# A decoder trunk layer in f32: the work up to the first Strassen pair in one fixed order on four engines, x transposed ahead of its modulation, w_ada summed two channel tiles at a time

## The chip, the cores and the metric

The kernel runs on one core of a Trainium2 chip. The core has TensorE (matrix products into PSUM banks), VectorE and ScalarE (elementwise work), GpSimd and SyncE, which here mostly issue loads and stores (SyncE the loads of weights and x, GpSimd small loads and the stores). In the profile they are PE (and PEld for its weight loads), DVE, ACT, POOL and SP. The metric is the device time of one execution in microseconds, as a median of several runs. Each profile belongs to one execution more, whose own time is given beside its span.

## What is computed

One layer, 1024 positions by 1024 channels, all in float32. Cut to what matters:

```python
mod = (c_act @ w_ada + b_ada)[:, None, :]
shift, scale, gate = jnp.split(mod, 3, axis=-1)
u = layer_norm(x) * (1 + scale) + shift
proj = u @ w_in + b_in
a_v, a_g, b_b, b_c, b_h, b_g, c_a, c_b, c_g, merge = jnp.split(proj, SPLIT_IDX, axis=-1)
...                       # three branches: pooling, short conv, conformer conv of 31 taps
h_c = causal_dwconv(c_a * jax.nn.sigmoid(c_b), cf_w, cf_b)
...
m = sum of sigmoid(merge_k) * (y_k @ w_branch[k])
return layer_norm(ALPHA * x + gate * (m @ w_out), ln_g, ln_b)
```

Everything starts at u: each of the 96 column tiles of the projection needs all of u, and u needs the normalised x and the first two thirds of c_act @ w_ada.

## The kernel before

**Precision.** A float32 product is made of three TensorE products of a coarser kind: an operand is split in a high half (a cast, `fp32r`) and a low half (the operand less its high half). `mm3` (L118) then adds low x high, high x low and high x high into one bank. So each operand costs a cast and a subtraction, "hi" and "lo" below. The cast is usually on ScalarE and the subtraction on VectorE (`split`, L109 to L111).

**u.** Channels lie on partitions. `ut[k]` is channel tile k (of 8) of the transposed, modulated x: 128 channels by 1024 positions, in two halves h of 512. `make_u` (L285) transposes four x tiles on TensorE into a bank (L288), and ScalarE writes `ut` from the bank with scale and bias of the modulation (L293). `split_u` (L297) makes hi (L301 on ScalarE, or L303, a cast on VectorE, by the table `HI_ACT`) and lo (L304) of it in `ub[k, h]`. The transposes and the small products of the modulation share two PSUM banks (`misc_ps`).

**The modulation.** `ada_load` brings w_ada in four pairs of channel tiles (a0, a2, a4, a6 in `LOADS`), each as four buffers of 512 KB. `ada_sum(k)` (L247) adds the eight row tiles, each times its c_act column, for one channel tile k: two starts on ScalarE (L257) and the rest on VectorE (L260, 256 columns, since shift and scale lie side by side). `ADA_PE` hands four of the eight rows of tile 0 to TensorE. `ada_mod(k)` (L270) sums over partitions with a product with ones (L276) and adds b_ada (L281).

**Jobs.** The projection's column tiles are jobs. The first four are *classic* jobs (class `Job`): 16 parts each (8 channel tiles, 2 halves), a part being one `mm3`, so 192 matmuls of 512 columns in all. All others are *pairs* (class `Pair`, L381): two column tiles at once as one step of Strassen-Winograd in seven products of twelve matmuls, A11·B11, A12·B21, S1·T1, S2·T2, S3·T3, S4·B22 and A22·T4. The S and A sides come from the weights (`prepare`, L398: four sums on VectorE and the splits wa, wb, wc, wd). The T sides are sums of quarters of u (`sum_u`, L308): four subtractions in place on `ut` (L312 to L315) and two splits, for each of four i. They can't begin before every split of those `ut` has been made. The first pair has the name b (its banks px_b, py_b, pz_b; its weights wa_b to wd_b), the next ones d and cg.

**The conv.** The two classic column-tile pairs end in `cs` (L482, L489), the input of the conformer conv: 30 instructions on VectorE for each of eight channel tiles (L519, the taps), six of them issued per job (`TAPS`).

**What sets the order.** `START` is a list of steps: l and n statistics and normalisation of an x tile, a and m the sum and the end of a modulation, u and v `make_u` and `split_u`, s a job's splits, p parts. It is read under `tc.manual_schedule(engines=PIN)` with `PIN` holding GpSimd alone. The other engines' orders are drawn by a scheduler while the kernel is built, from the order in the code and the dependencies, and are fixed from then on. Each engine works through its own list in that order and waits where an operand or a buffer isn't ready. The fourth classic job, the T sums and the first pair's splits follow START in the code (`ahead`, and `sum_u` ahead of the loop over jobs). Loads on SyncE's queue go in the order of `LOADS`, each as soon as its buffer is free; weights have four buffers (`RAW_BUFS`).

Of the kernel before, what the change touches and what calls it, by code (L numbers as in the profile page):

```python
# [46 lines left out]
def kernel(  # L47
# [117 lines left out]
    bin_cols = columns("bin_cols", [rows_of(b_in[0])], nc.gpsimd)  # L165
# [8 lines left out]
    vec_cols = columns("vec_cols", [a for _, a in names], nc.gpsimd)  # L174
# [11 lines left out]
    for i in range(2):  # L186
        sl = slice(i * nr, (i + 1) * nr)
        columns(f"cfw{i}", [cfw[sl, :]], nc.gpsimd, cfw_cols[:, sl])


    def rstd_of(name, var, n=1):
        r = small.tile([P, n], F32, tag=f"rstd{n}", name=name)
        nc.vector.tensor_scalar_add(r, var, EPS)
        nc.gpsimd.tensor_tensor(out=r, in0=r, in1=neg_half[:, :n], op=ALU.pow)
        return r
# [10 lines left out]

    def ln0_load(i):
        xn[i] = slot(f"x{i}")
        nc.sync.dma_start(out=xn[i], in_=x[i * P : (i + 1) * P, :])

    ln0_r = {}

    def ln0_stats(i):
        mv = stats_of(f"x{i}", xn[i])
        ln0_r[i] = mv, rstd_of(f"r{i}", mv[:, 1:2])

    def ln0(i):
        t, (mv, r) = xn[i], ln0_r[i]
        if i < 4:
            nc.vector.tensor_scalar(  # L220
                out=t, in0=t, scalar1=mv[:, 0:1], scalar2=r, op0=ALU.subtract, op1=ALU.mult
            )
            return
        nmr = small.tile([P, 1], F32, tag="nmr", name=f"nmr{i}")
        nc.vector.tensor_scalar(
            out=nmr, in0=mv[:, 0:1], scalar1=r, scalar2=-1.0, op0=ALU.mult, op1=ALU.mult
        )
        nc.scalar.activation(t, t, AF.Identity, bias=nmr, scale=r)
# [3 lines left out]
    def ada_load(k):  # L232

        for q in range(4):
            t = slot(f"ada{q}_{k}").rearrange("p (s k c) -> p s k c", s=2, c=2 * P)
            for s in range(2):
                marks["ada"] = nc.sync.dma_start(
                    out=t[:, s], in_=ada_src[:, s, 2 * q : 2 * q + 2, k * P : (k + 2) * P]
                )
            for e in range(2):  # L240
                raws.setdefault(k + e, []).extend(
                    t[:, :, i, e * P : (e + 1) * P] for i in range(2)
                )

    ada_acc = {}

    def ada_sum(k):  # L247

        raw, on_pe = raws[k], ADA_PE[k]
        parts = [(raw[kk], c_act[:, kk : kk + 1]) for kk in range(on_pe)]  # L250
        acc = []
        if on_pe < NT:
            both = slot(f"acc{k}").rearrange("p (n s c) -> p n s c", s=2, c=P)
        for kk in range(on_pe, NT):
            if len(acc) < 2:
                acc.append(both[:, len(acc)])
                nc.scalar.activation(acc[-1], raw[kk], AF.Identity, scale=c_act[:, kk : kk + 1])  # L257
            else:
                a = acc[(kk - on_pe) % 2]
                nc.vector.scalar_tensor_tensor(  # L260
                    out=a, in0=raw[kk], scalar=c_act[:, kk : kk + 1], in1=a,
                    op0=ALU.mult, op1=ALU.add,
                )
# [4 lines left out]
    mods = {}

    def ada_mod(k):  # L270

        ps = misc_ps(f"mod{k}")
        parts = ada_acc[k]
# [7 lines left out]
        nc.vector.tensor_add(mods[k], ps[:, :2], b)  # L281

    ut, ub = {}, {}

    def make_u(k, h):  # L285
        ps = misc_ps(f"tr{k}_{h}")
        for i in range(4):
            nc.tensor.transpose(  # L288
                ps[:, i * P : (i + 1) * P], xn[4 * h + i][:, k * P : (k + 1) * P], ident
            )  # L290
        if k not in ut:
            ut[k] = slot(f"ut{k}")
        nc.scalar.activation(  # L293
            ut[k][:, HALVES[h]], ps, AF.Identity, bias=mods[k][:, 0:1], scale=mods[k][:, 1:2]
        )

    def split_u(k, h):  # L297
        ub[k, h] = pair_slot(f"u{k}_{h}")
        hi, lo, t = ub[k, h][:, 0], ub[k, h][:, 1], ut[k][:, HALVES[h]]
        if HI_ACT[2 * k + h]:  # L300
            nc.scalar.activation(hi, t, AF.Identity)  # L301
        else:
            nc.vector.tensor_copy(out=hi, in_=t)  # L303
        marks["u"] = nc.vector.tensor_tensor(out=lo, in0=t, in1=f32(hi), op=ALU.subtract)  # L304
# [688 lines left out]
```

## Time and profile before

| | |
|---|---|
| median of the runs | 1421.26 us (3 runs, 1419.3 to 1421.34) |
| the profiled execution | 1417.33 us, its span 1415.6 us |
| busy in the span | PE 1335.6 (94%), DVE 1094.5 (77%), ACT 522.0 (37%), POOL 115.5 (8%) |
| mean granted TensorE clock | 0.986 |
| HBM read, written | 137.59 MB, 50.34 MB |

Two rows of the page show the span in 40 slices of 35.4 us. Each digit is the share of the slice in which the engine was busy, in tenths:

```profile
PE   2859999999999999999999999999998999999997
DVE  5589999999899769957985898699554757635576
```

TensorE is busy nine tenths and more in nearly every slice; the exceptions are the first three and a few later ones. VectorE is as busy as TensorE from the fourth slice to about the eleventh. The page adds busy times over stages that differ, so the prediction reads the first 230 us by themselves.

### The profile page before, as it was taken

To read this page: it belongs to the slowest core of one execution; us is meant where nothing else is said; L and a number is where in the kernel's file an instruction comes from. 1 tells how busy PE (TensorE), PEld (TensorE's weight loads), DVE (VectorE), ACT (ScalarE), POOL (GpSimd) and SP (SyncE) were. 2 spreads that over 40 slices of the span, in tenths; PEclk is the share of its full clock that TensorE was granted. 3 is DMA by queue.
4 is the path that set the end of the run, shared out by engine and by line. 5 is a ranking of instruction groups with operands and counts; after the bars stand their busy time and mean duration, and the time that the engine had idled before them with its cause. 6 is when DMAs were issued, how large, how long until landed. Compare 5 with 4: busy or idle time off the path is not lost.

```text
span 1415.6 us, 15312 instructions
## 1 busy us (share of the span) xinstructions
PE 1335.6 (94%) x5917; PEld 1100.9 (78%) x5917; DVE 1094.5 (77%) x1300; ACT 522.0 (37%) x654; POOL 115.5 (8%) x229
## 2 busy tenths in 40 slices
PE   2859999999999999999999999999998999999997
PEld 1647878888788878887888788877777888888886
DVE  5589999999899769957985898699554757635576
ACT  3453434443434434443444434344522333302200
POOL 3000000000000000000000000000211232200010
PEclk9989999999999999999999999999999999999998
DMA  9510222433312323221343224322777979812322
GB/s 333 148 45 16 75 89 90 134 107 102 119 60 75 104 75 104 77 89 44 105 149 104 80 76 133 113 89 82 272 273 275 333 270 359 288 63 64 130 102 92
DMA packets 168793, 188.92 MB, mean 133 GB/s; under 512 B 6420, under 2 KB 139616, under 8 KB 168720
## 3 DMA queue, kind: packets, MB, share of 16 engines
q1 hardware_dynamic: 142976, 95.43, 22.9%
q0 software_dynamic: 25696, 92.50, 17.4%
q8 instruction: 46, 0.75, 0.2%
q14 instruction: 27, 0.22, 0.0%
q10 hardware_dynamic: 48, 0.01, 0.0%
HBM read 137.59 MB, written 50.34 MB: 133 GB/s over the span
## 4 chain that ended last, share of the span: by engine, by line
PE 83%; issue 6%; DVE 5%; DMA 4%; ACT 2%; POOL 0%; SPq 0%; DVEq 0%; ACTq 0%; POOLq 0%
PE ps_z L120 17%; PE px_m L120 7%; PE px_d L120 6%; PE out_ps L120 6%; PE px_b L120 6%; PE px_a L120 5%; PE px_c L120 4%; PE pz_m L120 3%; PE px_cg L120 3%; PE pz_d L120 3%; PE pz_b L120 3%; PE ps_p L120 3%; PE pz_a L120 3%; PE pz_c L120 2%; DVE h L519 2%
## 5 line engine op out<-in xcount | busy, mean ns | idle before, releaser
L519 DVE SCALAR_TENSOR_TENSOR h<-r_c,cfw_cols,h 128x1023 f32<-128x1023 f32 (+9 forms) x180 | 227.1, 1262 | 5.1 <-ACT h L517 4.4
L741 DVE TENSOR_TENSOR g<-ps_z,g 128x512 f32<-128x512 f32 x48 | 31.8, 686 | 63.1 <-PE ps_z L120 62.5
L519 DVE SCALAR_TENSOR_TENSOR h<-cs,cfw_cols,h 128x1023 f32<-128x1023 f32 (+29 forms) x60 | 75.7, 1262 | 2.8 <-ACT h L517 2.3
L120 PE MATMUL ps_p<-u,w_p 128*128 128x512 f32 x192 | 52.6, 428 | 21.6 <-ACT cs L482 15.4
L110 ACT ACTIVATE w_z<-raw_z 128x1024 fp32r<-128x1024 f32 x24 | 25.2, 1060 | 123.2 <-PE ps_z L120 60.1
L120 PEld LDWEIGHTS ps_p<-u,w_p 128*128 128x128 f32 x192 | 37.9, 205 | 31.5 <-ACT cs L482 15.8
L111 DVE TENSOR_TENSOR w_z<-raw_z,w_z 128x1024 fp32r<-128x1024 f32 x24 | 29.1, 1220 | 18.7 <-ACT w_z L110 18.7
L120 PE MATMUL px_m<-u,wa_m 128*128 128x512 f32 x144 | 34.9, 390 | 2.5 <-DVE wa_m L111 2.5
L120 PE MATMUL ps_z<-y_1h,w_z 128*128 128x512 f32 x96 | 34.4, 394 | 2.0 <-ACT y_1h L115 2.0
L120 PE MATMUL px_m<-t_1h,wb_m 128*128 128x512 f32 x96 | 31.9, 392 | 4.5 <-ACT r_m L436 4.5
L120 PE MATMUL py_m<-u,wa_m 128*128 128x512 f32 x144 | 35.9, 389 | 0.0
L454 POOL DMA_DIRECT2D y_dram<-r_d x8 | 4.3, 539 | 379.4 <-DVE r_d L615 379.4
L120 PE MATMUL ps_z<-y_0h,w_z 128*128 128x512 f32 x96 | 35.2, 401 | 0.0
L120 PE MATMUL pz_m<-u,wc_m 128*128 128x512 f32 x144 | 35.1, 389 | 0.0
L120 PE MATMUL ps_z<-y_2h,w_z 128*128 128x512 f32 x96 | 33.9, 390 | 0.0
L120 PE MATMUL ps_z<-y_3h,w_z 128*128 128x512 f32 x96 | 33.7, 390 | 0.0
L120 PEld LDWEIGHTS px_m<-u,wa_m 128*128 128x128 f32 x144 | 27.0, 188 | 8.4 <-DVE wa_m L111 2.9
L120 PE MATMUL ps_z<-y_4h,w_z 128*128 128x512 f32 x96 | 33.5, 389 | 0.0
L120 PE MATMUL ps_z<-y_6h,w_z 128*128 128x512 f32 x96 | 33.5, 389 | 0.0
L120 PE MATMUL ps_z<-y_5h,w_z 128*128 128x512 f32 x96 | 33.5, 389 | 0.0
L120 PE MATMUL ps_z<-y_7h,w_z 128*128 128x512 f32 x96 | 33.1, 389 | 0.0
L120 PE MATMUL pz_m<-t_0h,wb_m 128*128 128x512 f32 x96 | 31.8, 389 | 0.0
(575 smaller groups left out, 3867.4 us busy)
## 6 DMA issues: line engine op xcount, KB each, us to landing
raw_m<-in_w_in_dram SPq DMA_DIRECT2D x24, 512.0 KB, 5.2
raw_z<-in_w_branch_dram SPq DMA_DIRECT2D x24, 512.0 KB, 8.3
g<-g_dram POOLq DMA_DIRECT2D x24, 512.0 KB, 7.7
g_dram<-r_m POOLq DMA_DIRECT2D x22, 512.0 KB, 3.3
ada<-in_w_ada_dram SPq DMA_DIRECT2D x32, 256.0 KB, 6.9
raw_b<-in_w_in_dram SPq DMA_DIRECT2D x16, 512.0 KB, 4.1
raw_d<-in_w_in_dram SPq DMA_DIRECT2D x16, 512.0 KB, 4.0
raw_a<-in_w_in_dram SPq DMA_DIRECT2D x16, 512.0 KB, 4.1
```

The lines of the kernel that those rows point to most:

```text
L110: nc.scalar.activation(hi, src, AF.Identity)
L111: marks["split"] = nc.vector.tensor_tensor(out=lo, in0=src, in1=f32(hi), op=ALU.subtract)
L120: nc.tensor.matmul(ps, w, r, start=start and n == 0, stop=stop and n == 2, skip_group_check=True)
L454: return (q or nc.gpsimd).dma_start(out=dst, in_=src)
L519: nc.vector.scalar_tensor_tensor(out=h[:, s:], in0=g[:, : S - s], scalar=w, in1=h[:, s:], op0=ALU.mult, op1=ALU.add,)
L741: nc.vector.tensor_mul(g[:, HALVES[h]], ps[h], g[:, HALVES[h]])
```

## The change

- **One list for four engines.** `PIN` now holds GpSimd, TensorE, VectorE and ScalarE, and `START` is written in single instructions: within it these four engines take their instructions in the list's order. The list reaches further than before. It holds all 64 parts of the four classic jobs (p, with job, channel tile and half), what ends the jobs (E), the T sums (Ta, Th, Tl) and all splits of the first pair (S12, S34, wah to wdl).
- **x transposed ahead of its modulation.** A transposed half is copied out of its bank as it is (t on TensorE, e on ScalarE). When the modulation is there, ScalarE writes hi from the copy with scale and bias (h), VectorE then modulates the copy in place (z) and subtracts (v). The casts on VectorE go; 16 modulations on VectorE come.
- **w_ada by two channel tiles.** The sums take 512 columns, for tiles k and k + 1 together: five or six instructions on VectorE for a pair, and always a join. TensorE takes two row tiles of the first pair.
- **Loads.** x0 to x3 come first, weights later, the order of SyncE's loads is held by dependencies, and the fourth job's weight is loaded once (before, it was loaded in LOADS and again by `ahead`). The first pair's weights are loaded ahead of START. The small loads of `bin_cols`, `vec_cols` and `cfw` move from GpSimd's queue to ScalarE's. Normalisations 4 to 7 stay on ScalarE; the power of the statistics is a step of its own (r).
- **Pairs.** In every pair A12·B21 with its evacuation moves up behind A11·B11, ahead of S1·T1.

```diff
-PIN = {ET.Pool}
+PIN = {ET.Pool, ET.PE, ET.DVE, ET.Activation}
-ADA_PE = (4, 0, 0, 0, 0, 0, 0, 0)
+ADA_PE = (2, 0, 0, 0)
+LN_ACT = (4, 5, 6, 7)
-LOADS = "w0 x0 x1 x2 x3 a0 x4 x5 x6 x7 a2 w1 w2 a4 w3 a6"
+LOADS = "x0 x1 x2 x3 a0 w0 x4 x5 x6 x7 w1 a2 w2 a4 a6 w3"
...
-    bin_cols = columns("bin_cols", [rows_of(b_in[0])], nc.gpsimd)
+    bin_cols = columns("bin_cols", [rows_of(b_in[0])], nc.scalar)
...
+    def ada_part(k, kk):
+
+        n = kk - ADA_PE[k // 2]
+        raw, scale = raws[k][kk], c_act[:, kk : kk + 1]
+        if n < 2:
+            acc[k, n] = slot(f"acc{n}_{k}")[:, : 4 * P].rearrange("p (s c) -> p s c", s=2)
+            nc.scalar.activation(acc[k, n], raw, AF.Identity, scale=scale)
+        else:
+            a = acc[k, n % 2]
+            nc.vector.scalar_tensor_tensor(
+                out=a, in0=raw, scalar=scale, in1=a, op0=ALU.mult, op1=ALU.add
+            )
+
+    def ada_join(k):
+        nc.vector.tensor_add(acc[k, 0], acc[k, 0], acc[k, 1])
...
+    def evacuated(k, h):
         if k not in ut:
             ut[k] = slot(f"ut{k}")
+        nc.scalar.copy(ut[k][:, HALVES[h]], tr[k, h])
+
+    def high_u(k, h):
+        ub[k, h] = pair_slot(f"u{k}_{h}")
         nc.scalar.activation(
-            ut[k][:, HALVES[h]], ps, AF.Identity, bias=mods[k][:, 0:1], scale=mods[k][:, 1:2]
+            ub[k, h][:, 0], ut[k][:, HALVES[h]], AF.Identity,
+            bias=mods[k][:, 0:1], scale=mods[k][:, 1:2],
         )
+    def make_u(k, h):
+        t = ut[k][:, HALVES[h]]
+        nc.vector.tensor_scalar(
+            out=t, in0=t, scalar1=mods[k][:, 1:2], scalar2=mods[k][:, 0:1],
+            op0=ALU.mult, op1=ALU.add,
+        )
+
+    def low_u(k, h):
+        marks["u"] = nc.vector.tensor_tensor(
+            out=ub[k, h][:, 1], in0=ut[k][:, HALVES[h]], in1=f32(ub[k, h][:, 0]), op=ALU.subtract
+        )
...
             self.product(px, "A11", "B11", True)
             nc.scalar.activation(r1[:, LEFT], px, AF.Identity, bias=bias(col1))
+            py = bank(f"py_{self.name}")
+            self.product(py, "A12", "B21", True)
+            nc.vector.tensor_add(r1[:, LEFT], py, r1[:, LEFT])
             self.product(pz, "S1", "T1", True)
...
-    n_first = 0
+    jobs[CLASSIC].load()
+    marks["started"] = True
...
-    prepared = {i for i in range(3)}
-    loaded = {i for i in range(3)}
+    prepared = set(range(CLASSIC + 1))
+    loaded = set(range(CLASSIC + 1))
...
-    for i in range(NT // 2):
-        sum_u(i)
     c_stage()
```

How the engines' lists move shows at three places. The first is VectorE's list where the first channel tiles of u are split. In the names, u_0 and u_1 are the halves of a channel tile's split, ut the transposed x, acc a w_ada sum, mod a modulation. Before:

```order
L281 TENSOR_TENSOR mod_444<-mod_441,ada_cols 128x2
L304 TENSOR_TENSOR u_0_456<-ut_451,u_0_456 128x512
L304 TENSOR_TENSOR u_1_471<-ut_385,u_1_471 128x512
L260 SCALAR_TENSOR_TENSOR acc_480<-ada_2_275,c_act,acc_480 128x256 x2
L260 SCALAR_TENSOR_TENSOR acc_480<-ada_2_278,c_act,acc_480 128x256
L304 TENSOR_TENSOR u_1_492<-ut_451,u_1_492 128x512
```

After the change, in the same place:

```order
L310 TENSOR_TENSOR mod_494<-mod_474,ada_cols 128x2
L335 TENSOR_SCALAR ut_390<-ut_390,mod_483 128x512
L341 TENSOR_TENSOR u_0_487<-ut_390,u_0_487 128x512
L335 TENSOR_SCALAR ut_419<-ut_419,mod_494 128x512
L341 TENSOR_TENSOR u_0_497<-ut_419,u_0_497 128x512
L285 SCALAR_TENSOR_TENSOR acc_2_505<-ada_2_277,c_act,acc_2_505 128x512
L285 SCALAR_TENSOR_TENSOR acc_2_505<-ada_2_280,c_act,acc_2_505 128x512
```

Each half now takes two instructions of VectorE where it took one, and the w_ada sums run over 512 columns.

The second place is VectorE's list at the fourth job's weight (w_p_898 before, w_p_843 after) and the first pair's splits (s_b and wa_b); t_0l and t_1l are low halves of T sums. Before:

```order
L314 TENSOR_TENSOR ut_664<-ut_664,ut_626 128x512
L314 TENSOR_TENSOR ut_775<-ut_775,ut_706 128x512
L111 TENSOR_TENSOR w_p_898<-raw_p_890,w_p_898 128x1024
L412 TENSOR_TENSOR s_b_917<-raw_b_0_894,s_b_916 128x512
L111 TENSOR_TENSOR wa_b_918<-raw_b_0_894,wa_b_918 128x1024
L315 TENSOR_TENSOR ut_451<-ut_451 128x512
```

After the change:

```order
L354 TENSOR_TENSOR ut_426<-ut_426 128x512
L362 TENSOR_TENSOR t_1l<-ut_447,t_1h 128x1024
L362 TENSOR_TENSOR t_0l<-ut_399,t_0h 128x1024
L362 TENSOR_TENSOR t_0l<-ut_445,t_0h 128x1024
L362 TENSOR_TENSOR t_1l<-ut_426,t_1h 128x1024
L409 TENSOR_TENSOR w_p_843<-raw_p_312,w_p_843 128x1024
L573 SCALAR_TENSOR_TENSOR cs_833<-ps_p_0_508,bin_cols,cs_833 128x512
L573 SCALAR_TENSOR_TENSOR cs_833<-ps_p_1_509,bin_cols,cs_833 128x512
L503 TENSOR_TENSOR wa_b_852<-raw_b_0_314,wa_b_852 128x1024
```

The T sums of three of the four i now stand ahead of the fourth job's weight and the last of them behind the first pair's splits; the scheduler had drawn all of the subtractions together.

The third place is TensorE's list at the end of the fourth job (ps_p with w_p_898 before, w_p_843 after) and the first products of the pair. Before:

```order
L120 MATMUL ps_p_1_935<-u_1_777,w_p_898 128x512 x3
L120 MATMUL ps_p_0_934<-u_0_789,w_p_898 128x512 x3
L120 MATMUL ps_p_1_935<-u_1_825,w_p_898 128x512 x3
L120 MATMUL px_b_1014<-u_0_387,wa_b_918 128x512 x3
L120 MATMUL px_b_1014<-u_0_558,wa_b_918 128x512 x3
L120 MATMUL px_b_1014<-u_0_628,wa_b_918 128x512 x3
L120 MATMUL px_b_1014<-u_0_762,wa_b_918 128x512 x3
L120 MATMUL pz_b_1015<-t_0h,wb_b_923 128x512
```

After the change:

```order
L132 MATMUL ps_p_0_863<-u_0_692,w_p_843 128x512 x3
L132 MATMUL ps_p_0_863<-u_0_737,w_p_843 128x512 x3
L132 MATMUL px_b_988<-u_0_487,wa_b_852 128x512 x3
L132 MATMUL px_b_988<-u_0_692,wa_b_852 128x512 x3
L132 MATMUL px_b_988<-u_0_687,wa_b_852 128x512 x3
L132 MATMUL px_b_988<-u_0_728,wa_b_852 128x512 x3
L132 MATMUL py_b_1005<-u_0_497,wa_b_852 128x512 x3
L132 MATMUL py_b_1005<-u_0_600,wa_b_852 128x512 x3
L132 MATMUL py_b_1005<-u_0_670,wa_b_852 128x512 x3
L132 MATMUL py_b_1005<-u_0_737,wa_b_852 128x512 x3
L132 MATMUL pz_b_989<-t_0h,wb_b_893 128x512
```

Twelve matmuls that need only u and wa now stand between A11·B11 and the first product with a T. Of the list START itself the diff shows nothing here; it names 64 parts, 16 transposes and what goes with them.

More of the change, by code (lines that the diff above doesn't have):

```diff
@@ L268 @@
[L268 to L273 removed]
+                marks["ada"] = in_order(
+                    nc.sync.dma_start(
+                        out=t[:, s], in_=ada_src[:, s, 2 * q : 2 * q + 2, k * P : (k + 2) * P]
+                    )
+                )
+            raws.setdefault(k, []).extend(t[:, :, i] for i in range(2))
+    acc = {}
+    def ada_part(k, kk):
[4 more added lines that the diff above has]
+            nc.scalar.activation(acc[k, n], raw, AF.Identity, scale=scale)
+        else:
+            a = acc[k, n % 2]
+            nc.vector.scalar_tensor_tensor(
+                out=a, in0=raw, scalar=scale, in1=a, op0=ALU.mult, op1=ALU.add
+            )
@@ L274, in ada_mod @@
+    def ada_join(k):
+        nc.vector.tensor_add(acc[k, 0], acc[k, 0], acc[k, 1])
+    mods, mod_ps = {}, {}
+    def ada_mod(k):
+        even = k // 2 * 2
+        ks = slice((k - even) * P, (k - even + 1) * P)
+        ps = mod_ps[k] = misc_ps(f"mod{k}")
+        parts = [(raws[even][kk], c_act[:, kk : kk + 1]) for kk in range(ADA_PE[k // 2])]
+        parts.append((acc[even, 0], ones[:, 0:1]))
         for s in range(2):
@@ new lines, in step @@
+            which, high = what[1], what[2] == "h"
+            if high and which == "d":
+                self.w[which] = wlast.tile([P, 2, HALF], F32R, tag="last", name=f"wd_{self.name}")
+            elif high:
+                self.w[which] = wspl.tile([P, 2, D], F32R, tag="w", name=f"w{which}_{self.name}")
+            hi, lo = (self.w[which][:, n] for n in range(2))
+            if which == "d":
+                src = a2[:, 1]
+                hi, lo = (t.rearrange("p (i c) -> p i c", c=P) for t in (hi, lo))
+            else:
+                src = raw1 if which == "a" else self.sums["1" if which == "b" else "3"]
@@ L424, in product @@
+            if high:
+                nc.scalar.activation(hi, src, AF.Identity)
+            else:
+                marks["split"] = nc.vector.tensor_tensor(
+                    out=lo, in0=src, in1=f32(hi), op=ALU.subtract
+                )
         def product(self, ps, left, right, first):
-            w, block = self.left[left]
+            which, block = self.left[left]
+            w = self.w[which]
             for i in range(4):
```

207 lines of the change are left out of this document (102 added, 105 removed), and 12 rows, old and new, of the table START.

## The prediction, made before the changed kernel was run

> **What bounds the kernel now.** I read the chain that ended last, then busy time by stage, then the waits.
>
> ```profile
> PE 83%; issue 6%; DVE 5%; DMA 4%; ACT 2%; POOL 0%; SPq 0%; DVEq 0%; ACTq 0%; POOLq 0%
> ```
>
> TensorE carries 83% of the chain, so the end moves only where TensorE is held up. The stages show where that is (columns: stretch, length, then busy us of PE, PEld, DVE, ACT, POOL, the granted clock, DMA share, GB/s):
>
> ```profile
> 0.00:30.00 30.00, 7.29 (x29) 6.12 (x30) 19.45 (x46) 8.24 (x14) 10.57 (x41) 1.00 1.00 330
> 30.00:60.00 30.00, 21.96 (x87) 16.66 (x88) 14.88 (x38) 14.70 (x24) 0.78 (x2) 0.94 0.83 237
> 60.00:86.00 26.00, 25.49 (x146) 21.40 (x146) 16.67 (x41) 13.70 (x23) 0.00 (x0) 1.00 0.00 1
> 86.00:107.00 21.00, 6.00 (x27) 4.64 (x25) 21.00 (x30) 11.01 (x12) 0.00 (x0) 0.76 0.26 75
> 107.00:120.00 13.00, 12.64 (x49) 10.36 (x50) 11.54 (x12) 3.29 (x5) 0.00 (x0) 0.87 0.01 2
> 120.00:230.00 110.00, 107.11 (x465) 88.19 (x465) 105.45 (x111) 44.65 (x55) 2.21 (x4) 0.98 0.22 68
> ...
> 119.00:600.00 481.00, 476.58 (x2088) 391.93 (x2087) 438.87 (x470) 199.76 (x246) 14.98 (x28) 1.00 0.29 89
> ```
>
> After 119 us TensorE works 476.58 of 481 us. Before that VectorE idles half of the time up to 86 us (24.5 of 56 us between 30 and 86) and is then the only busy engine for 21 us, while TensorE waits. The chain in order of time and the longest wait of TensorE say the same (start, us, what):
>
> ```profile
> 106.62 0.70 ACT cs L482
> 107.36 12.61 PE ps_p L120 x48
> 119.97 2.72 PE px_b L120 x12
> ```
> ```profile
> PE ps_p L120 <- ACT cs L482: 15.4, 1, 15.4
> ```
>
> The fourth classic job (48 matmuls) starts only at 107.36, after the T sums, and the first pair at **119.97 us**. A product of a pair is 12 matmuls, 2.72 us; a part of a classic job is three, 0.68 us. What follows the first pair is nearly the same work in both kernels, so the question is how much earlier the pair starts, and whether VectorE keeps up with it afterwards.
>
> **Prices on VectorE.** Its queue turns out to set the new start, so its instructions are priced from start to start (start, us, instruction):
>
> ```profile
> 82.81 0.43 DVE L303 CAST u<-ut 128x512 fp32r<-128x512 f32 x1 [0.39 <-ACT ut L293]
> 83.27 1.29 DVE L304 TENSOR_TENSOR u<-ut,u 128x512 fp32r<-128x512 f32 x2
> ...
> 85.92 2.49 DVE L312 TENSOR_TENSOR ut<-ut 128x512 f32<-128x512 f32 x4
> 88.33 0.68 DVE L408 TENSOR_TENSOR s_b<-raw_b 128x512 f32<-128x512 f32 x1
> ...
> 110.52 1.22 DVE L111 TENSOR_TENSOR t_1l<-ut,t_1h 128x1024 fp32r<-128x1024 f32 x1
> 111.65 1.40 DVE L489 SCALAR_TENSOR_TENSOR cs<-ps_p,bin_cols,cs 128x512 f32<-128x512 f32 x2
> ...
> 126.87 5.20 DVE L519 SCALAR_TENSOR_TENSOR h<-cs,cfw_cols,h 128x1016 f32<-128x1016 f32 x4
> ...
> 133.72 1.26 DVE L519 SCALAR_TENSOR_TENSOR h<-cs,cfw_cols,h 128x1012 f32<-128x1012 f32 x1
> 134.91 1.22 DVE L111 TENSOR_TENSOR wb_d<-s_d,wb_d 128x1024 fp32r<-128x1024 f32 x1
> ```
>
> A two-tensor operation of 512 columns costs 0.60 (2.41 / 4), of 1024 columns 1.13, a cs operation 0.70, a conv tap 1.19 with another operation behind it and up to 1.30 in a run of taps (5.20 / 4); I take 1.24. The new modulation of u in place (one tensor, two column operands, 512 columns) is not in the trace. It lies between the cast, 0.46 with its reader right behind, and a two-tensor operation, 0.68; I take 0.46, since the cast too reads one tensor. A w_ada sum of 512 columns is not there either: 0.60 to 0.70 by its neighbours; I take 0.65.
>
> **The change, part by part.**
>
> *w_ada by two channel tiles.*
>
> ```profile
> L260 DVE SCALAR_TENSOR_TENSOR acc<-ada,c_act,acc 128x256 f32<-128x256 f32 x44 | 18.7, 476 | 1.3 <-ACT acc L257 1.3
> ```
>
> 44 instructions become 22 (4 x 5 or 6, less the shares on TensorE) of 0.65, with four joins of 0.60 for two of 0.42: some 16.7 us for 18.8, 2 us less. Four casts go (0.33 to 0.46 each), sixteen modulations come (7.4 us). VectorE's whole work up to the pair therefore grows by about 4 us; what the change removes is its idle time.
>
> *First part of a classic job.* Two lists set it. VectorE's begins with c_act, four statistics and four normalisations:
>
> ```profile
> 9.45 0.17 DVE L161 TENSOR_TENSOR c_act<-ada_cols,c_sig 128x8 f32<-128x8 f32 x1 [0.28 <-ACT c_sig L159]
> ```
> ```profile
> L200 DVE BATCH_NORM_STATS2 st_x<-x 128x6 f32<-128x512 f32 x16 | 10.0, 676 | 1.5 <-DMA x<-in_x_dram 1.5
> L220 DVE TENSOR_SCALAR x<-x,mv_x,r 128x1024 f32<-128x1024 f32 x4 | 3.2, 808 | 1.3 <-POOL r L194 1.2
> ```
>
> c_act stood behind two high halves of weights on ScalarE (1.05 each), which now come later: 7.4. Eight statistics of 0.68, four normalisations of 0.81 and some 1.2 of small ones make 9.9, less about 0.1 where each overlaps the next: 16.5 us, with x leading the loads. ScalarE then has eight copies of transposes, two high halves of weights, four normalisations, two starts of sums and the first high half of u:
>
> ```profile
> L293 ACT ACTIVATE ut<-tr,mod 128x512 f32<-128x512 f32 x16 | 12.1, 770 | 20.6 <-DVE mod L281 11.7 <-PE tr L288 8.9
> L301 ACT ACTIVATE u<-ut 128x512 fp32r<-128x512 f32 x12 | 7.5, 625 | 0.2
> L228 ACT ACTIVATE x<-x,nmr,r 128x1024 f32<-128x1024 f32 x4 | 4.6, 1230 | 8.8 <-DVE nmr L225 8.8
> L110 ACT ACTIVATE w_p<-raw_p 128x1024 fp32r<-128x1024 f32 x4 | 4.2, 1049 | 2.7 <-DMA raw_p<-in_w_in_dram 2.7
> ```
>
> 8 x 0.77 + 2 x 1.05 + 4 x 1.23 + 3 x 0.63 = 15.1, less 0.1 for each overlap and with a little for the two banks that the transposes pass back and forth: 14.5. The first part is at **31 us**; the rows allow 28 to 33. The small loads that ScalarE now issues stand ahead of these in its queue; they cost nothing if they have landed by 16.5.
>
> *VectorE from 31 us to the last T sum.* Its new list holds 16 modulations (7.4), 42 two-tensor operations of 512 (25.3), 18 w_ada sums (11.7), 13 of 1024 columns (14.8), four cs operations (2.8) and six small ones (0.6): 62.6 us, so the last low half of T is written at 93.6 if it never waits. Loads don't hold it:
>
> ```profile
> 33.21 6.68 SPq L237 DMA_DIRECT2D ada<-in_w_ada_dram  x8
> ```
> ```profile
> ada<-in_w_ada_dram SPq DMA_DIRECT2D x32, 256.0 KB, 6.9
> ```
>
> The last w_ada pair was issued by 39.9 and landed about 6.9 us later, at 46.8, with as much ahead of it on SP's queue as now; VectorE reaches it at about 47. The first pair's weights follow it, without the second load of the fourth job's weight between, and are used after 70. The next pair's second weight waits for the fourth job's buffer: free at about 77, landed 7 us later at 84, wanted at about 86; what it is later than that, VectorE waits.
>
> *TensorE in the same stretch.* 64 parts (43.5), seven groups of transposes (0.45 each) and the small products (1.5) are 48.6 us: 79.6 at the earliest. But up to the last low half of u it is paced by VectorE: 21.3 us of its list up to the last w_ada join, 10.9 for the last ten modulations and splits, so 63.2. Behind that stand 18 parts of the first three jobs and 16 of the fourth, 23.1 us, and half a part: the pair starts at about **87 us**. A11 and A12 need no T, 5.4 us more, and at 92.4 the first T1 quarter is just written. The 15.4 us wait is gone, and nothing stands in its place there; also gone are the 1.7 us by which the fourth job ran slow (12.61 for 48 x 0.227).
>
> *Behind the pair.* Before, VectorE had five conv taps (6.4 us) done at the pair; now none. Its list is fixed, so I add it up to where TensorE presses hardest: the splits of the second cg pair's wa, 103 instructions after the last T half. 42 taps (52.1), 41 of 512 (24.7), 20 of 1024 (22.8): 99.6 us, so 193.2. TensorE gets there after 38 products, 87 + 103.4 = 190.4. **VectorE is the bound over this stretch**, not TensorE. For its waits on ScalarE I add 3 us: between zero and the 4.6 us of idle that it had in 120 to 230 us; the 24.5 us between 30 and 86 are the upper end. So 196.2. Before, 38 products after the first pair ended at 119.97 + 103.4 + 2.9 + 1.9 = 228.2, by a wait and a slow product:
>
> ```profile
> 188.14 4.60 PE L120 MATMUL px_d<-u,wa_d 128*128 128x512 f32 x12 [2.89 <-DVE wa_d L111]
> ```
>
> The gain is 228.2 - 196.2 = **32 us**. Behind that I change nothing. Span 1415.6 - 32 = 1383.6; around the span lies 1.7 (1417.3 in all), so 1385.3 for that execution. The median of the runs shown is 3.9 us above it: **1389**.
>
> **Rivals.**
>
> *TensorE sets the start.* If VectorE's modulations and taps cost the lower bounds (taps 1.19: 2 us less; sums 0.60: 1 us; no waits: 3 us) and the first half of u comes at 28, TensorE runs through: pair at about 79.6, and the 4.8 us of later waits gone too: 45 us gained, 1376. For it: VectorE waited only 4.6 us in 110 once its queue was full. Against: it needs every order of four engines to fit.
>
> *More waiting, or a half clock, between 31 and 63 us.* VectorE idled 24.5 us in 56 in this kind of work. And TensorE slowed after a short pause:
>
> ```profile
> 53.00:56.00 3.00, 0.81 (x5) 0.42 (x4) 1.69 (x5) 2.73 (x6) 0.00 (x0) 0.96 0.00 1
> 56.00:60.00 4.00, 3.92 (x14) 3.30 (x15) 4.00 (x11) 0.82 (x3) 0.00 (x0) 0.60 0.00 0
> ```
>
> Granted clock 0.60 over 4 us costs 1.6 us, and the new order has waits for VectorE all along. If the clock stayed at half there, 33 parts would take 44.9 us instead of 22.4, less some 4.6 us of waiting: the pair 16 to 18 us late, a gain of 16 to 20 us in all, about 1403. Eight us of further waits on VectorE alone give 1397. [...] By the row one or two spells come, 1.6 us each, most of it inside TensorE's waiting for VectorE.
>
> *Slower.* From 119 to 600 us VectorE idled 42.1 us (481 - 438.87), mostly for ScalarE, and TensorE only 4.4: VectorE was far enough ahead. Now it starts six taps behind and the whole later order is drawn anew. If all of that idle time reaches TensorE, 37.7 us are lost and the time is 1427. It decides once more than 35 of those 42 us are passed on. Against it: the list leaves VectorE 4 to 10 us ahead of TensorE again some 40 us behind the tight place.
>
> *No effect.* If the list did not do what it says (T sums still ahead of the fourth job), the 15.4 us wait would stay. VectorE's list has them apart; this needs another wait of equal size.
>
> **How the numbers follow.** Forecast, VectorE's queue sets the stretch, 1380 to 1397: 0.60. TensorE sets it, 1370 to 1380: 0.14. More waits or half clock, 1397 to 1410: 0.18. Slower, 0.04; no effect, 0.04. A measurement of this kernel tells 0.2% (2.8 us) from no change. Faster 0.92, within 0.2% 0.04, slower 0.04. The range 1376 to 1404 leaves out half of the second case, a third of the third and the last two, a little under 0.2.
>
> **What the profile would show.** First part at 31 us; VectorE busy nine tenths and more from 31 on; no wait of the fourth job for a cs; first product of the pair at about 87 us, its T1 product at 92; the tightest wait of TensorE on a low half of wa or wb at 150 to 200 us. A first product before 82 or after 92, or a gap of VectorE of over 5 us between 31 and 90, would show which step is off. The prediction is wrong if ScalarE's small loads hold its queue beyond 17 us, if modulations cost more than 0.7, or if TensorE's waits after 200 us differ by more than 6 us from before.

## The result, and the profile after

| | before | after |
|---|---|---|
| median of the runs | 1421.3 us (4 runs, 1419.3 to 1422.9) | 1390.0 us (4 runs, 1389.4 to 1390.3) |
| ratio, 95% interval | | 0.978 (0.976 to 0.980) |
| the profiled execution, its span | 1417.3, 1415.6 us | 1390.3, 1388.6 us |
| busy PE, DVE, ACT | 1335.6, 1094.5, 522.0 us | 1329.0, 1100.0, 528.0 us |

The kernel is 31 us faster; the profiled executions lie 27.0 us apart. The same stretches of the program as before, after the change (stretch, length, then busy us of PE, PEld, DVE, ACT, POOL, the granted clock, DMA share, GB/s):

```profile
0.00:30.00 30.00, 11.01 (x48) 7.50 (x48) 19.12 (x44) 12.22 (x21) 7.33 (x32) 0.94 0.87 285
30.00:60.00 30.00, 25.27 (x122) 20.25 (x123) 28.25 (x51) 20.01 (x29) 1.58 (x1) 0.83 0.91 265
60.00:86.00 26.00, 24.16 (x105) 18.30 (x104) 25.49 (x39) 15.23 (x20) 0.00 (x0) 1.00 0.03 8
86.00:107.00 21.00, 21.00 (x95) 17.36 (x94) 20.52 (x26) 8.43 (x9) 0.00 (x0) 1.00 0.24 70
120.00:230.00 110.00, 100.96 (x438) 82.79 (x437) 103.15 (x109) 43.96 (x55) 2.85 (x5) 0.97 0.27 82
```

VectorE works 53.7 of the 56 us between 30 and 86 us, where it worked 31.6 before, and TensorE no longer stands still between 86 and 107. But from 120 to 230 us TensorE now works 101 us, where it worked 107. Its timeline shows the first part, the fourth job and the first pair (start, us, instruction, and in brackets the idle time before it and its releaser):

```profile
35.41 2.04 PE L132 MATMUL ps_p<-u,w_p 128*128 128x512 f32 x3
...
83.86 11.22 PE L132 MATMUL ps_p<-u,w_p 128*128 128x512 f32 x48 [0.95 <-DVE w_p L409]
94.92 2.88 PE L132 MATMUL px_b<-u,wa_b 128*128 128x512 f32 x12
97.64 2.88 PE L132 MATMUL py_b<-u,wa_b 128*128 128x512 f32 x12
100.36 0.39 PE L132 MATMUL pz_b<-t_0h,wb_b 128*128 128x512 f32 x1
```

The fourth job's wait of 15.4 us is gone, the pair starts at 94.92 us instead of 119.8, and its T1 product (pz_b) follows without a wait. TensorE's waits behind 85 us, grouped (us in total, times, longest):

```profile
PE pool_ps L132 <- ACT pool6h L127: 10.1, 1, 10.1
PE px_b L132 <- ACT r_b L520: 5.9, 1, 5.9
PE pz_d L132 <- DVE wb_d L503: 3.1, 1, 3.1
PE pool_ps L132 <- ACT pool0h L127: 1.7, 1, 1.7
PE ps_z L132 <- ACT y_3h L127: 1.1, 1, 1.1
```

Three waits are new or larger: for wb_d at 168.9 us, for an eviction r_b at 177.9, and 10.1 us for a reloaded tile of the pool stage, pool6, at about 1062 (4.0 before).

**Where the gain lies.** I compare at four points with equal TensorE work in between: the first product of the first pair, the end of 38 products from there (103.4 us of work), the first product of the output stage, and the end. The table also holds the runs below. Times are of the profiled execution of each, in us. (Before, the pair's first matmul starts at 119.81; the prediction's 119.97 is where the chain's step begins.)

| kernel | pair | +38 products | output stage | span | median |
|---|---|---|---|---|---|
| before | 119.8 | 228.0 | 1317.4 | 1415.6 | 1421.3 |
| after | 94.9 | 209.6 | 1290.7 | 1388.6 | 1390.0 |
| t_sums_later | 112.6 | 229.1 | 1319.8 | 1418.0 | 1417.2 |
| old_products | 93.8 | 211.7 | 1298.1 | 1396.0 | 1398.7 |
| drawn_order | 107.9 | 215.6 | 1294.7 | 1392.6 | 1392.8 |
| pe_extra | 99.6 | 213.2 | 1291.8 | 1389.8 | 1391.3 |
| dve_extra | 94.1 | 214.9 | 1290.4 | 1388.3 | 1389.2 |
| hsum_dve | 94.2 | 202.8 | 1277.0 | 1374.8 | 1376.5 |
| taps_later | 93.9 | 197.2 | 1273.8 | 1371.7 | 1374.0 |
| z_on_act | 98.1 | 211.8 | 1289.4 | 1387.2 | 1390.2 |
| taps_and_small | 91.8 | 195.1 | 1273.2 | 1371.4 | 1374.0 |

(In taps_later and taps_and_small the second point is the pair's start plus 38 x 2.72, since TensorE doesn't wait up to there.) The change gains 24.9 us up to the pair, gives 6.5 back in the next 38 products, and gains 8.6 behind them: 27.0.

The wait for pool6 differs by 6 us between these kernels, and the traces show what sets it. In each of them 13.7 to 14.2 us lie between TensorE's last product with the tile pool5 and its first with pool6. In that time VectorE gates the result, GpSimd stores it and then issues the reload of pool6 (3.3 us after the product with pool5), the reload lands 9.3 to 9.8 us later, and ScalarE casts it. TensorE fills this time with what the drawn order has put there: 18 matmuls in the change and in pe_extra (4.1 us, so it waits 10.1), 25 or 26 where the wait is 8 us, 43 where it is 4, as in the kernel before.

One execution of the run small_on_pool, the profiled one, had TensorE at half rate (matmuls of 512 columns start 0.45 us apart instead of 0.23; span 2732.4 us); the comparison leaves it out, and what its edit does is read in taps_and_small, which holds it too.

### The profile page after: what moved, and what is told of

It reads as the page before. It is cut to its first block, busy times and chain, and to the rows that moved or that the text cites. A ratio compares the mean times of both kernels' runs of the same rounds, so it can differ in the third digit from the quotient of the medians.

```text
span 1388.6 us, 15235 instructions
## 1 busy us (share of the span) xinstructions
PE 1329.0 (96%) x5893; PEld 1093.3 (79%) x5893; DVE 1100.0 (79%) x1292; ACT 528.0 (38%) x652; POOL 113.7 (8%) x220
## 3 DMA queue, kind: packets, MB, share of 16 engines
q1 hardware_dynamic: 141936, 94.91, 23.1%
## 5 line engine op out<-in xcount | busy, mean ns | idle before, releaser
L538 POOL DMA_DIRECT2D g_dram<-r_m x22 | 11.7, 533 | 349.3 <-ACT r_m L713 238.0
L132 PE MATMUL px_m<-u,wa_m 128*128 128x512 f32 x144 | 34.8, 389 | 0.0
L1027 DVE TENSOR_TENSOR og<-out_ps,gate_b 128x512 f32<-128x512 f32 (+1 forms) x18 | 11.1, 624 | 26.6 <-PE out_ps L132 13.4
L132 PE MATMUL px_m<-t_0h,wc_m 128*128 128x512 f32 x96 | 31.5, 389 | 0.0
```

Source lines behind the costliest of these rows:

```text
L132: nc.tensor.matmul(ps, w, r, start=start and n == 0, stop=stop and n == 2, skip_group_check=True)
L538: return (q or nc.gpsimd).dma_start(out=dst, in_=src)
L1027: nc.vector.tensor_mul(t, ps[q], final["gate"][:, sl])
```

## The experiments

All but the first are edits of the changed kernel. Ratios are against the kernel before, with 95% intervals.

**t_sums_later: in the kernel before, the T sums are emitted behind the third job.**

```diff
-    for i in range(NT // 2):
-        sum_u(i)
     c_stage()
...
         job.run()
+        if i == 2:
+            for n in range(NT // 2):
+                sum_u(n)
```

> The kernel before with one edit: the T sums are emitted behind the third classic job instead of ahead of the whole job loop, nothing else. Theory A (the 15.4 us wait of the fourth job behind the T sums is the main loss of the kernel before, and the start up to there is a second, smaller one): in VectorE's list the cs operations and the fourth job's low half now stand some 17 instructions behind the last u split, so the fourth job starts at about 97 to 98 us instead of 107.4, the pair at about 109 instead of 120, the T1 product then waits 2 to 3 us: 8 to 11 us gained, about 1411 us. Theory B (the wait is only where VectorE's queue shows, its length is the sum of the work ahead; taking it away there moves it to the T1 product): T1 is asked for at 112 and comes no earlier than before, the pair waits there for most of it, gain under 3 us, 1418 to 1421.

0.998 (0.997 to 0.999), 1417.2 us; the kernel before had 1420.2 beside it. TensorE's waits from 85 to 230 us:

```profile
PE ps_p L120 <- DVE w_p L111: 6.7, 1, 6.7
PE px_b L120 <- ACT r_b L436: 6.2, 1, 6.2
PE px_d L120 <- DVE wa_d L111: 3.4, 1, 3.4
```

The edit takes away 8.7 of the 15.4 us and not the whole wait: in VectorE's drawn list 12 of the 16 T subtractions still stand ahead of the fourth job's low half (w_p). The pair starts 7.2 us earlier, and after 38 products all of it is lost (229.1 against 228.0). B's size is nearly right, but not its place: T1 follows at once, and the wait comes later, where TensorE needs what VectorE has yet to do. The new 6.2 us for r_b stand behind ScalarE's copy of hsum, which waits 9.18 us for a tap at 189.0, the place that hsum_dve takes up below. I read the 15.4 us as the sign of the loss, and VectorE's idle time ahead of 86 us, which this edit leaves as it was (busy 14.9 of 30 and 16.5 of 26 us), as the loss itself. A run that takes away the whole wait and nothing else is missing.

**old_products: the pair's seven products in the old order.**

```diff
             self.product(px, "A11", "B11", True)
             nc.scalar.activation(r1[:, LEFT], px, AF.Identity, bias=bias(col1))
-            py = bank(f"py_{self.name}")
-            self.product(py, "A12", "B21", True)
-            nc.vector.tensor_add(r1[:, LEFT], py, r1[:, LEFT])
...
             nc.scalar.activation(r1[:, RIGHT], px, AF.Identity, bias=bias(col1))
+            py = bank(f"py_{self.name}")
+            self.product(py, "A12", "B21", True)
+            nc.vector.tensor_add(r1[:, LEFT], py, r1[:, LEFT])
```

> The changed kernel with the products of a pair in the old order (A12 x B21 behind S2 x T2). Theory A (behind the first pair VectorE's list and ScalarE's evictions set the pace, 9 us of TensorE's waits at 168 and 177 us): the first pair starts at 95 us as before this edit, its T1 product is asked for at 97.6 and waits 2 to 3 us until 100.3, and the two waits behind it shrink by as much: the end moves by under 1.5 us, 1389 to 1392. Theory B (TensorE sets the pace behind the pair): the end moves by the whole 2.7 us or more, 1393 to 1396.

0.985 (0.983 to 0.987), 1398.7 us: 8.7 us slower than the change, more than either theory. Its waits behind 85 us:

```profile
PE px_b L132 <- ACT r_b L520: 6.4, 1, 6.4
PE pool_ps L132 <- ACT pool6h L127: 4.1, 1, 4.1
PE px_a L132 <- DVE wa_a L503: 3.5, 1, 3.5
PE px_m L132 <- ACT r_m L520: 3.4, 2, 1.8
PE px_d L132 <- DVE wa_d L503: 2.9, 1, 2.9
PE px_m L132 <- DVE wa_m L503: 2.5, 1, 2.5
```

The waits for wa_a, wa_m and r_m stood in the kernel before (3.5, 2.5 and 4.5 us), and with the new order of products none of them is left. Against that, the wait for pool6 is 4.1 us here and 10.1 in the change, so the numbers that follow are net of 6 us; these hang on the drawn order and not on the products, for hsum_dve has the new order of products and waits 4.1. Though its pair starts 1.1 us earlier, the kernel is 2.1 us behind after 38 products, and 5.3 us more are lost behind them. As measured, the order of products is thus worth about a quarter of the whole gain, and most of that lies far behind the first pair.

**drawn_order: only GpSimd is held to the list.**

```diff
-PIN = {ET.Pool, ET.PE, ET.DVE, ET.Activation}
+PIN = {ET.Pool}
```

> The changed kernel with only GpSimd held to the list; the scheduler draws the order of TensorE, VectorE and ScalarE from the same steps. Theory A (the gain comes from the fixed order): the drawn list puts T sums between the u splits and the fourth job's low half behind the last of them, so the pair starts 6 to 12 us later than 94.9 and the time is 1396 to 1403. Theory B (the new data flow with x transposed ahead gives the gain, whatever the order): pair within 3 us of 94.9, 1387 to 1393.

0.981 (0.979 to 0.982), 1392.8 us: 2.8 slower than the change. Half of each theory holds. The drawn order puts the pair 13.0 us later, as A said and more; the time is B's. After 38 products 6.0 us of the 13.0 are left, since TensorE's only wait up to there is 2.4 us for wb_d, against 9.0 in the change. VectorE's idle time is mostly gone in this kernel too (busy 23.1 of 30 and 26.0 of 26 us). The new steps, as they stand in the code, bring most of the gain; holding four engines to that order adds 2.8 us. Which of the steps brings it isn't shown: apart from the order of products and the small loads, no run takes one of them back alone (x transposed ahead, the sums over two tiles, the order of the loads).

**pe_extra and dve_extra: more work on one engine.** 24 matmuls ahead of the pair on TensorE, or eight operations on VectorE behind the last T half:

```diff
-... p370 wch E3 T0h0 wcl T0h1 T0l0 T0l1
+... p370 wch E3 T0h0 wcl T0h1 T0l0 T0l1 q24
+            nc.tensor.matmul(
+                ps, jobs[3].w[:, 0, :P], ub[7, 1][:, 0], start=i == 0, stop=i == n - 1
+            )
```
```diff
-... p370 wch E3 T0h0 wcl T0h1 T0l0 T0l1
+... p370 wch E3 T0h0 wcl T0h1 T0l0 T0l1 q8
+            nc.vector.tensor_tensor(out=spare, in0=spare, in1=spare, op=ALU.subtract)
```

> The changed kernel with 24 further matmuls of 512 columns on TensorE right ahead of the first pair (5.4 us, their result is read by nobody). Theory A (behind the pair VectorE's list sets the pace up to some 200 us, and TensorE's 9.0 us of waits at 168 and 177 us are where it waits for that list): the pair starts 5.4 us later, at 100.4, these waits shrink by as much, and the products from 200 us on start at the same time as without: 1389 to 1391. Theory B (TensorE sets the pace, the start of the pair passes on to the end): 1394 to 1396.

> The changed kernel with eight further operations of 512 columns on VectorE (8 x 0.60 to 0.73, 4.8 to 5.8 us) right behind the last low half of T, on columns that nobody reads any more. Theory A (VectorE's list is the bound from there to some 200 us): every wait of TensorE in that stretch comes so much later, the end moves by 4 to 6 us: 1394 to 1396. Theory B (VectorE has room there): 1389 to 1391.

0.980 (0.979 to 0.982), 1391.3 us, and 0.979 (0.977 to 0.980), 1389.2 us. By their times the first looks like A and the second like B. The points of the table say something else. After 38 products pe_extra is 3.7 us behind the change (of 4.7 at the pair), and dve_extra 5.3, though its pair starts 0.8 earlier (8 x 0.60 = 4.8 were put in, and came to stand spread among the instructions behind the T halves). In pe_extra the waits up to there shrink from 9.0 to 5.6 us, as its theory A says, but TensorE loses 4.6 us at half clock behind them (granted clock 0.50 from 180 to 185 us, matmuls 0.43 us apart instead of 0.23), where the change loses 2.2 (0.50 from 175 to 180; 4.7 - 3.4 + 2.4 = 3.7). In dve_extra the waits grow to 12.6 us and the half clock (0.50 from 180 to 185 us) costs 4.7 (3.6 + 2.5 - 0.8 = 5.3). So VectorE's delay passes on, while TensorE's is mostly taken up by its waits, and what remains of it is about the clock's share. TensorE's long waits are, in pe_extra:

```profile
PE pool_ps L132 <- ACT pool6h L127: 10.1, 1, 10.1
PE px_b L132 <- ACT r_b L520: 3.2, 1, 3.2
PE pz_d L132 <- DVE wb_d L503: 2.4, 1, 2.4
```

and in dve_extra:

```profile
PE px_b L132 <- ACT r_b L520: 9.7, 1, 9.7
PE pool_ps L132 <- ACT pool6h L127: 4.2, 1, 4.2
PE pz_d L132 <- DVE wb_d L503: 2.9, 1, 2.9
```

In dve_extra the delay of 5.3 us is made good 850 us later, where the wait for pool6h falls from 10.1 to 4.2 us; in pe_extra 2.5 us come back far behind the 38 products too. So the end alone misleads here: the order behind START is drawn anew in each kernel, and its late part shifts by several us.

**taps_later: 21 conv taps leave the stretch up to 200 us.**

```diff
-            conv_step(TAPS if i < n_proj - 1 else NT * K31)
+            conv_step((3 if i < 9 else TAPS) if i < n_proj - 1 else NT * K31)
```

> The changed kernel with three conv taps instead of six behind each of the jobs 2 to 8, so that 21 taps (26 us of VectorE) leave the stretch up to some 230 us and are made up behind later jobs. Theory A (VectorE's list bounds the stretch from the pair to 200 us): the waits of TensorE at 168 and 177 us (3.1 and 5.9) go, 6 to 9 us gained against the changed kernel, 1381 to 1384, and the later waits don't grow by over 2 us. Theory B (the waits come from ScalarE's order or from loads): 1388 to 1391.

0.969 (0.967 to 0.970), 1374.0 us: 16 us faster than the change. TensorE waits for nothing between the pair and the pool stage:

```profile
PE pool_ps L132 <- ACT pool6h L127: 8.2, 1, 8.2
PE pool_ps L132 <- ACT pool0h L127: 1.7, 1, 1.7
PE ps_z L132 <- DVE y_3l L128: 0.5, 1, 0.5
```

Between the pair and the 38th product some 11 us go: the two waits of 9.0 us, and 2.2 that TensorE lost behind them at half clock. Theory A holds for the place; the time lies 7 us below its range. Of the rest, 1.1 us lie ahead of the pair, where the list is the same (the first part came 0.9 earlier in this execution), and 4.5 in later, redrawn parts, 1.9 of them in the wait for pool6.

**hsum_dve: one copy from ScalarE to VectorE.**

```diff
-                    nc.scalar.copy(conv["sum"], h)
+                    nc.vector.tensor_copy(out=conv["sum"], in_=h)
```

> The changed kernel with the copy of the first finished convolution tile (hsum) on VectorE instead of ScalarE. In the changed kernel ScalarE's copy waits 9.3 us for VectorE's last tap at 176.2, and the eviction of the pair's first product stands behind it: TensorE waits 5.9. Theory A (that place in ScalarE's list is the wait): the 5.9 us go down to under 1, and 3 to 6 us of it reach the end, 1384 to 1387. Theory B (the copy only marks VectorE's lateness, which comes through at the next split): the wait goes to a low half behind it, 1388 to 1391.

0.970 (0.968 to 0.972), 1376.5 us: 13.5 faster. The place, on ScalarE's timeline of the changed kernel:

```profile
176.17 1.04 ACT L615 COPY hsum<-h 128x1024 f32<-128x1024 f32 x1 [9.28 <-DVE h L605]
177.12 0.68 ACT L520 ACTIVATE r_b<-px_b,bin_cols 128x512 f32<-128x512 f32 x1
```

The copy waits 9.28 us for VectorE's last tap, and the eviction that TensorE needs stands behind it. With the copy moved TensorE's wait for r_b is gone; the one for wb_d stays (3.1). After 38 products the kernel is 6.8 us ahead, as A says. Nearly all of the rest, by which the time lies below A's range, is the wait for pool6h, 4.1 instead of 10.1, in a part that the edit doesn't touch.

**small_on_pool: the small loads back on GpSimd's queue.**

```diff
-    bin_cols = columns("bin_cols", [rows_of(b_in[0])], nc.scalar)
+    bin_cols = columns("bin_cols", [rows_of(b_in[0])], nc.gpsimd)
...
-        columns(f"cfw{i}", [cfw[sl, :]], nc.scalar, cfw_cols[:, sl])
+        columns(f"cfw{i}", [cfw[sl, :]], nc.gpsimd, cfw_cols[:, sl])
```

> The changed kernel with the small column loads (bin_cols, vec_cols, cfw) issued by GpSimd again, as before the change. In the changed kernel SP issues the first load of x only at 3.68 us, and its wait is put down to a small load of ScalarE's queue. Theory A (the small loads hold up SP's first loads, and this is why the first part came at 35.4 and not at 31): x is issued at about 0.75, VectorE's first statistics start at 4.4 to 6, the first part comes 2.5 to 3 us earlier, and since VectorE's list sets the rest, pair and end move by the same: pair at about 92, 1386 to 1388. Theory B (the first part hangs on ScalarE's own list and on the transfer of the weights): first part within 1 us of 35.4, time within 1 us of 1390.

0.974 (0.972 to 0.976), some 1384 us: 6 faster than the change. In the changed kernel SyncE's first loads, and the waits that its queue shows:

```profile
3.68 5.18 SPq L231 DMA_DIRECT2D x<-in_x_dram  x4
```
```profile
SPq L231 <- DMA vec_cols_rows<-in_cf_b_dram: 3.5, 1, 3.5
SPq L231 <- DMA vec_cols_rows<-in_pool_scale_dram: 3.0, 1, 3.0
```

and with the edit (taps_and_small), the loads and the first part on TensorE:

```profile
0.75 1.80 SPq L231 DMA_DIRECT2D x<-in_x_dram  x4
2.59 6.56 SPq L268 DMA_DIRECT2D ada<-in_w_ada_dram  x8
```
```profile
32.31 2.04 PE L132 MATMUL ps_p<-u,w_p 128*128 128x512 f32 x3
```

The first load of x waits 3.0 us, a later one 3.5. Theory A holds for the start: the first part is 3.1 us earlier than in the change and so is the pair (91.75); against taps_later, from which taps_and_small differs by this edit alone, the two are 2.2 and 2.1 us earlier. For the other 3 us of this run there is an estimate: its list has 31 matmuls ahead of pool6 where the change has 18, and 13 x 0.227 makes 2.9 us. No trace at full rate shows it.

**z_on_act: the modulations in place are done by ScalarE.**

```diff
-        nc.vector.tensor_scalar(
-            out=t, in0=t, scalar1=mods[k][:, 1:2], scalar2=mods[k][:, 0:1],
-            op0=ALU.mult, op1=ALU.add,
-        )
+        nc.scalar.activation(
+            t, t, AF.Identity, bias=mods[k][:, 0:1], scale=mods[k][:, 1:2]
+        )
```

> The changed kernel with the sixteen modulations in place on ScalarE instead of VectorE, nothing else. Theory A (VectorE's list sets the stretch from the first part to the pair): its list is 16 x 0.57 = 9.1 us shorter, ScalarE's some 12 us longer in a stretch where it idles 22 of 56 us; the last T half is written at 92 to 94 instead of 101, the pair starts 4 to 6 us earlier than 94.9 (then TensorE's own work is the bound), and the waits behind it, which hang on VectorE, come 7 to 9 us earlier: 1381 to 1386. Theory B (ScalarE's list, in which a modulation now stands between two high halves, becomes the bound): pair not before 94, 1388 to 1393.

0.980 (0.977 to 0.982), 1390.2 us, no difference that these runs can tell. Theory B: the pair comes 3.2 us later, at 98.1, though VectorE has 9 us less to do. Its stretches from 30 and from 60 us:

```profile
30.00:60.00 30.00, 23.10 (x112) 17.33 (x112) 23.35 (x38) 23.37 (x35) 1.49 (x1) 0.89 0.90 262
60.00:86.00 26.00, 22.66 (x96) 17.68 (x94) 18.84 (x28) 20.60 (x27) 0.00 (x0) 0.93 0.00 1
```

VectorE idles 13.8 of 56 us again (2.3 in the change). ScalarE, at 44 of 56 us, works through its own list in order, and VectorE waits for it. In the change ScalarE works 35 and VectorE 54 of these 56 us.

**Three together.** taps_and_small holds taps_later and small_on_pool; taps_small_z adds z_on_act to these, taps_small_hsum adds hsum_dve.

> Three taps behind the jobs 2 to 8 and the small loads on GpSimd together. Theory A: with the taps away nothing but TensorE's own work lies between the pair and 200 us (33 products in 89.8 us), so the 3 us of the earlier first part reach the end in full: pair at about 91, 1369 to 1372. Theory B (the 5.6 us that the small loads alone gave came from a luckier order behind 230 us, not from the start): pair at 91, but the end anywhere from 1372 to 1378.

> The same two edits and the modulations on ScalarE. Theory A: pair at 85 to 87, T ready by 88 to 91, no wait behind it up to 200 us: 1364 to 1368. Theory B (ScalarE becomes the bound ahead of the pair): within 2 us of the two edits alone.

> The two edits (taps, small loads) and the copy of the first convolution tile on VectorE. Theory A (both edits, of the taps and of the copy, take away the same wait at 177 us): no gain over the two edits up to 230 us; whatever differs comes from the pool stage, where pool6h was waited for 10.1 us in the changed kernel and 4.1 with the copy moved: 1366 to 1372. Theory B (they add up): 1360 to 1363.

1374.0, 1377.5 and 1373.8 us; ratios 0.968 (0.966 to 0.970), 0.970 (0.969 to 0.972), 0.968 (0.966 to 0.970). The small loads make the pair of taps_later 2.1 us earlier, and nothing of it reaches the end: theory B. The modulations on ScalarE cost 3.5 us here, which neither theory had. The copy adds nothing once the taps are moved, as A says: both took away the same wait. That the time lies 2 us above A's range fits the wait for pool6, 8.2 us here, which A had hoped to see at 4.1. taps_later, taps_and_small and taps_small_hsum don't differ enough to rank them; each beats both kernels, the change by some 16 us.

## Why the prediction was right, point by point

The forecast of 1389 was met within 1 us (1390.0), by errors that cancel, so its closeness is luck. The case that it named as likeliest is the one that came: VectorE's list sets the stretch up to the second cg pair. Behind the pair taps_later and dve_extra show it; ahead of the pair it rests on the trace alone (53.7 us busy of 56), since z_on_act, which shortens VectorE's list there, made ScalarE the late one.

- **First part at 31 us: 35.4, outside its rows' 28 to 33.** The failing sentence is that the small loads on ScalarE's queue "cost nothing if they have landed by 16.5". They had, and ScalarE lost nothing by them behind that, but SyncE's loads of x waited for two of them (3.0 and 3.5 us above). That explains 2.2 to 3.1 us. In the other kernels with the same list up to there the first part came at 34.3 to 34.8, so 0.6 to 1.1 us are this execution's own; for the remaining 1.3 (32.3 in taps_and_small against 31) I have no run.
- **VectorE from 31 us on, 62.6 us without a wait.** From the first modulation at 34.91 to the end of the last T half at 101.26 it is 66.4 us, nearly without idle (53.7 busy of 56, 20.5 of 21 us). The mechanism is right, the prices too low where an instruction reads what the one before it wrote, or overwrites what that one read:

```profile
34.91 0.55 DVE L335 TENSOR_SCALAR ut<-ut,mod 128x512 f32<-128x512 f32 x1 [0.75 <-ACT u L328]
35.49 0.69 DVE L341 TENSOR_TENSOR u<-ut,u 128x512 fp32r<-128x512 f32 x1
36.10 0.54 DVE L335 TENSOR_SCALAR ut<-ut,mod 128x512 f32<-128x512 f32 x1
...
52.77 3.77 DVE L285 SCALAR_TENSOR_TENSOR acc<-ada,c_act,acc 128x512 f32<-128x512 f32 x5
...
70.42 0.69 DVE L352 TENSOR_TENSOR ut<-ut,ut 128x512 f32<-128x512 f32 x1
71.15 0.69 DVE L353 TENSOR_TENSOR ut<-ut,ut 128x512 f32<-128x512 f32 x1
```

  The modulation takes 0.58 from start to start (35.49 - 34.91; I took 0.46, the lower bound), a w_ada sum in a run 0.75 (3.77 / 5; 0.65), a T subtraction behind its forerunner 0.73 (71.15 - 70.42; 0.60).
- **Pair at 87: 94.9.** 4.4 from the first part, the rest from these prices: the fourth job's weight, behind them in VectorE's list, is what TensorE waits for at 83.86. The prediction had named a first product after 92 us as a sign that a step was off, and these two are the steps. The steps behind are right: 11.2 us of the fourth job, two products, and no wait for T1 at 100.4 (92.4 plus the same lateness).
- **VectorE from the last T half to the second cg pair's wa, 99.6 and 3 us of waits.** It is 105.4 (101.3 to 206.7), of which 6.8 are six waits of 0.6 to 1.8 us: the work was sized right, at 98.6, the waits were twice the 3 that I added. TensorE starts that pair at 209.55 us where I had 196.2. Of the 13.4 us, 7.7 come from the later start of VectorE's list, 2.8 from its longer run, and 2.9 because TensorE was later still: the wait of 5.9 us hangs on ScalarE's place in line (hsum_dve), and half clock costs 2.2 more. "VectorE is the bound, not TensorE" was half right: taps_later shows that its work sets the waits, and in pe_extra a later TensorE waits 3.4 us less. But the longest wait came of ScalarE's order, and the half clock behind the waits stood at nothing in this sum.
- **"Behind that I change nothing."** This failed the other way: 8.6 us were gained there. TensorE's waits behind the 38 products sum to 20.1 us before and 14.9 after: 12.0 for r_m, wa_a, wa_m and r_d are gone, and 6.1 more go to pool6. The other 3.4 us are matmuls that ran slower than 0.227 us (5.0 us before, 1.6 after). old_products gives 5.3 of the 8.6, net of the pool6 wait, to the order of products, which I had priced at the first pair alone. I had looked at what A12 needs, and not at which waits the same edit takes away in all the other pairs.
- **The median 3.9 us above the profiled execution.** So it is for the kernel before, but the profiled execution of the changed one, 1390.3, lies at its median. The account by spans is 32 forecast and 27.0 measured; without the 3.9 the forecast would have been 1385.
- **Rivals.** TensorE sets the start: no, the pair came at 94.9 (its 48.6 us of TensorE's work are 48.2 by their own terms; nothing hangs on that). Slower, by VectorE's later waits: these grew, as the rival says, but TensorE lost 6.5 us by them up to the 38th product, and not 37.7. A half clock between 31 and 63 us: it came (granted clock 0.83 over 30 to 60; matmuls start 0.43 us apart instead of 0.23 at 36.8, 44.7 and 47.2 us, two or three each time) and cost next to nothing. old_products runs the same list up to the pair, with the clock at 1.00 in that stretch: 59.4 us from its first part (34.49) to its pair (93.84), where the change has 59.5, and taps_later, at 0.81, has 59.3.

**The clock behind a wait.** I had weighed a row, a pause of 2.18 us with the clock at 0.60 behind it. The first matmuls behind this pause start 0.43 us apart instead of 0.23, and six of them take 2.72 us (58.80 - 56.08):

```profile
56.08 2.93 PE L120 MATMUL ps_p<-u,w_p 128*128 128x512 f32 x6 [2.18 <-ACT u L301]
58.80 0.42 PE L276 MATMUL mod<-ones,acc 128*128 128x1 f32 x2
```

Here is hsum_dve around its only wait in the stretch, 3.1 us at 168.1 (PE busy, clock, DMA share, GB/s):

```profile
160.00:170.00 10.00, 6.90 (x30) 0.96 0.35 109
170.00:175.00 5.00, 5.00 (x18) 0.73 0.00 0
```

The clock fell after 3.10 us, and in pe_extra after 2.42 (0.75 over the 5 us from 170). Not each such pause did it: in the change, behind 3.10 us at 168.9, the matmuls start 0.23 us apart from the second on, and only behind the 5.94 us at 177.85 do they start 0.43 apart, for 3 us. So these runs show no length of a pause that decides. The spell in hsum_dve cost some 2 us (108.6 - 103.4 - 3.1 = 2.1).

## What to carry to other kernels

A long wait on one engine names the place where a queue runs dry, not the loss: look for the idle time of the engine that is late there, since taking away 8.7 of its 15.4 us gave 3 of 31 us. Where several in-order engines feed each other, look for the instruction that waits for a slow engine while another's release stands behind it in line; moving one copy, or 21 instructions that nobody wants yet, was worth about half as much here as the whole change. Judge such an edit at points of equal TensorE work, since a redrawn order far behind can give or take 6 us of its own.

## What the runs showed of the hardware that I had not expected

- The first load on SyncE's queue waited 3.0 us for a small load of another queue, with nothing ahead of it on its own, and a later one 3.5; with the small loads on GpSimd's queue the first was issued at 0.75 us instead of 3.68.
- In the change an instruction of 512 columns on VectorE took 0.11 to 0.13 us longer, from its start to the next one's, if the next read its result: a modulation 0.58 against 0.46, a w_ada sum 0.78 against 0.67. So did a T subtraction if the next read its result or overwrote what it had read, 0.73 against 0.60.
- GpSimd's reload of pool6 landed 9.3 to 9.8 us after its issue in thirteen traces (9.8 in the change, where the eight loads of the like tile hc took 5.9 to 9.4). With what stands around it TensorE needs 14 us of other work between two such tiles, and the order of the change gives it 4.1.
